# A hybrid decoder block: the causal mask inside the stick-breaking scan, and the short convolution summed by chunk in PSUM

## The chip, the cores and the metric

The kernel runs on one core of a Trainium2 chip. The metric is the device time of one launch in microseconds; the time of a version is the median of its plain runs, and one further run is taken with the profiler on. Engines are called TensorE (PE in the profile; PEld is its weight load), VectorE (DVE), ScalarE (ACT), GpSimd (POOL) and SyncE (SP, which only issues DMAs here). SBUF is the on-chip memory, PSUM the eight banks into which TensorE writes.

## The reference, cut to what matters

One decoder layer on 1,024 tokens plus 16 meta tokens, width 1,024, all in float32. The part that the change touches:

```
xn = rms_norm(h)
b, c, hh, q, k, v, g_conv, g_attn = split(xn @ w_in)
y_conv = b * causal_dwconv(c * hh, conv_w_mix)        # 3 taps per channel
# attention, per head, blocks of queries, keys s < t only:
z        = q k^T / 8
log_fail = where(s < t, log_sigmoid(z) - z, 0)        # log(1 - sigmoid(z))
survive  = cumsum of log_fail from the right, exclusive
a        = where(s < t, exp(log_sigmoid(z) + survive), 0)
o        = a @ v
merged = sigmoid(g_conv + b0) * (y_conv @ w_proj_conv) + sigmoid(g_attn + b1) * (o @ w_proj_attn)
h = h + rms_norm(merged @ w_out)
```

Then a gated MLP, whose up-projection passes through a second causal depthwise convolution of three taps, and `h = h + rms_norm(mlp)`. In products, an attention weight is `sigmoid(z_ts)` times all `1 - sigmoid(z_tj)` for `s < j < t`; so the kernel takes `fl = sigmoid(-z)`, a running product of it from the right, and `be = sigmoid(z)`.

## The kernel before

**Stages.** A first stretch (to about 60 us) normalises the tokens and transposes them into `xnT` (features on partitions). The long second stage, to about 985 us, interleaves two kinds of work. Third, the rest of the gates, the two branch projections, the output projection; fourth, the MLP. Every float32 product is made of three products in the rounded format `float32r` (high by high, high by low, low by high), so operands are split in two: ScalarE casts the high half (L64), and VectorE, or GpSimd for weights, subtracts it for the low half (L65). The operand names ending in `hi`/`lo` or `h`/`l` are these halves.

**Dense items** (class `Dense`). An item is a block of 128 output columns of `w_in`, computed for three chunks of 342 token columns. A chunk is 24 matmuls (L124 to L126) into one PSUM bank of the pool `ps_mm`, which has three banks under the tag `mm`; then its `evac` function takes the result out. When an item starts, the weights of the next one are split: cast on ScalarE, subtraction on GpSimd (`wlo`). The weights after that are loaded by SP. Per head pair the items are `c`, `h`, `b` (the convolution branch: `items_conv`), one gate, and `v`, `q`, `k` of the next pair.

**The convolution.** `evac_c` (L272) copies `c` to SBUF, `evac_h` (L276) multiplies it chunk by chunk with `h` straight from PSUM, and after the third chunk `conv3` (L196 to L198) runs over all 1,026 columns at once, in SBUF: one ScalarE pass with the weight of the third tap, and two VectorE passes `yy = cc * w + yy` for the other two. `evac_b` (L283) multiplies `yy` by `b` and stores it.

**Attention** runs in units of a pair, a head and three blocks of 114 queries. `stage1` makes the scores of a block (L325, L326; up to three pieces of PSUM), the two sigmoids on ScalarE (L327 for `fl`, L328 for `be`), and one step later calls `weights`: VectorE sets the `fl` of masked keys to 1 by a maximum with the tile `ones_up` over the last 114 columns (L335), and scans the block from the right (L336: state = fl * state, minimum with fl). GpSimd multiplies `be` by the scanned `fl`, shifted by one (L338), zeroes the masked part (L339) and pads (L344). `stage2` transposes the weights by TensorE into two PSUM banks called `tp` (L372), splits them into `ah` (ScalarE) and `al` (VectorE), and multiplies by the values (L362, L363). At its end the two halves of the sum are added: ScalarE copies one to `otmp` (L389), VectorE adds (L390). The values are transposed through the same `tp` banks, split into `vv`.

**What sets the order.** A loop written by hand takes steps of `stage1` and `stage2` by planned costs and spends dense steps between them in proportion, so TensorE's order is fixed in advance. On each engine instructions run in the order of its queue, and the compiler's scheduler may place an instruction of another stream between two of the source. Tiles come from pools with a fixed number of buffers; a tile waits until its buffer's last user is done.

**Small tiles.** `par` holds per-channel constants, 106 columns: convolution weights of the mixer (24), gate biases (16) and convolution weights of the MLP (66). It is loaded on SP after the first tokens and weights (L471). The first stretch takes its scalars from a pool `p0s` with four buffers. In the output projection SP loads `g_post` (L683) and `g_pre` (L684), and VectorE multiplies each product by `g_post` (L712).

Of the kernel before, what the change touches and what calls it, by code (L numbers as in the profile page):

```python
# [8 lines left out]
F32 = mybir.dt.float32  # L9
F32R = mybir.dt.float32r  # L10
AF = mybir.ActivationFunctionType
ALU = mybir.AluOpType
PSUM = bass.MemoryType.PSUM

P = 128
# [4 lines left out]
NT = 1040  # L20
NQ = NT - T0
CH = NQ // 3
# [10 lines left out]
def block_kernel(ctx, tc, x, meta_tokens, g_pre_mix, w_in, channels, w_proj_conv,  # L33
# [4 lines left out]
    def pool(name, bufs=1, side="left", space=None):  # L38
        kw = dict(name=name, bufs=bufs, reuse_waits="tile")
        if space is not None:  # L40
            kw["space"] = space
        else:
            kw["side"] = side
        return tc.tile_pool(**kw)
# [3 lines left out]

    ident = const.tile([P, P], F32, name="ident")
    make_identity(nc, ident)  # L50
    par = const.tile([P, 106], F32, name="par")

    o_d = tc.dram_tile([D, NQ], F32, name="o_d")
    y_d = tc.dram_tile([D, NQ], F32, name="y_d")
# [100 lines left out]
    def col_block(w, c):  # L155
# [9 lines left out]
    xnt_ctx = ctx.enter_context(ExitStack())  # L165
    xnt_pool = xnt_ctx.enter_context(pool("xnt"))
    xnT = xnt_pool.tile([P, 2, KB, NT], F32R, name="xnT")
    ones_up = xnt_pool.tile([QB, QB], F32, name="ones_up")
    nc.gpsimd.memset(ones_up, 0.0)
    nc.gpsimd.affine_select(out=ones_up, in_=ones_up, pattern=[[-1, QB]], compare_op=ALU.is_gt,  # L170
                            fill=1.0, base=0, channel_multiplier=1)

    def to_features(dst_hi, dst_lo, src, n, pp):
        for j in range(2):
# [11 lines left out]
    def w_mix(k, b):  # L186
        return par[:, k * 8 + b:k * 8 + b + 1]
# [2 lines left out]
        return par[:, 24 + k * 8 + b:24 + k * 8 + b + 1]  # L190

    def w_ffn(k, b):
        return par[:, 40 + k * NFF + b:40 + k * NFF + b + 1]

    def conv3(dst, src, n, wt):
        nc.scalar.activation(dst, src[:, 2:2 + n], AF.Copy, scale=wt(2))  # L196
        nc.vector.scalar_tensor_tensor(dst, src[:, 1:1 + n], wt(1), dst, op0=ALU.mult, op1=ALU.add)
        nc.vector.scalar_tensor_tensor(dst, src[:, 0:n], wt(0), dst, op0=ALU.mult, op1=ALU.add)  # L198
# [67 lines left out]
    def items_conv(cb):  # L266
        st = {}

        def evac_c(ci, a, n, ps):
            if ci == 0:  # L270
                st["c"] = work.tile([P, NT], F32, name="cc", tag="wk", bufs=4)
            nc.scalar.copy(st["c"][:, a - 12:a - 12 + n], ps)  # L272

        def evac_h(ci, a, n, ps):
            c = st["c"][:, a - 12:a - 12 + n]
            nc.vector.tensor_tensor(c, c, ps, op=ALU.mult)  # L276
            if ci == 2:
                st["y"] = work.tile([P, NT], F32, name="yy", tag="wk", bufs=4)
                conv3(st["y"][:, :NQ], st["c"], NQ, lambda k: w_mix(k, cb))

        def evac_b(ci, a, n, ps):
            y = st["y"][:, a - T0:a - T0 + n]
            nc.vector.tensor_tensor(y, y, ps, op=ALU.mult)  # L283
            if ci == 2:
                nc.sync.dma_start(y_d[cb * P:(cb + 1) * P, :], st["y"][:, :NQ])

        return [(col_block(w_in, 8 + cb), src_x, CH_C, evac_c),
                (col_block(w_in, 16 + cb), src_x, CH_C, evac_h),
                (col_block(w_in, cb), src_x, CH_Q, evac_b)]
# [20 lines left out]
    def stage1(p, h, g):  # L310
# [3 lines left out]
        for b in range(3 * g, 3 * g + 3):  # L314
# [17 lines left out]
                if c0 < nk:  # L332
                    yield n
            def weights(fl=fl, be=be, nk=nk):
                nc.vector.tensor_tensor(fl[:, nk - QB:nk], fl[:, nk - QB:nk], ones_up, op=ALU.max)  # L335
                nc.vector.tensor_tensor_scan(fl[:, :nk][:, ::-1], fl[:, :nk][:, ::-1],  # L336
                                             fl[:, :nk][:, ::-1], 1.0, op0=ALU.mult, op1=ALU.min)
                nc.gpsimd.tensor_tensor(be[:, 0:nk - 1], be[:, 0:nk - 1], fl[:, 1:nk], op=ALU.mult)  # L338
                nc.gpsimd.affine_select(out=be[:, nk - QB:nk], in_=be[:, nk - QB:nk],  # L339
                                        pattern=[[-1, QB]], compare_op=ALU.is_gt, fill=0.0,  # L340
                                        base=0, channel_multiplier=1)
                pad = min(P * (-(-nk // P)), nk_end)
                if pad > nk:
                    nc.gpsimd.memset(be[:, nk:pad], 0.0)  # L344
# [7 lines left out]
    def stage2(p, h, g):  # L352
# [31 lines left out]
        if (h, g) == (0, 0):  # L384
            OT[p] = work.tile([P, NT], F32, name="ot", tag="wk", bufs=4)
        ot = OT[p]
        tmp = work.tile([P, CH], F32, name="otmp", tag="otmp")
        a, b = (0, 64) if h == 0 else (64, 0)
        nc.scalar.copy(tmp[a:a + 64], av[b:b + 64])  # L389
        nc.vector.tensor_tensor(ot[a:a + 64, CH * g:CH * (g + 1)], av[a:a + 64], tmp[a:a + 64],  # L390
                                op=ALU.add)
        if (h, g) == (1, 2):
            nc.sync.dma_start(o_d[p * P:(p + 1) * P, :], ot[:, :NQ])
        yield unit
# [32 lines left out]
        chunk(1, 9)  # L427

    with ExitStack() as p0:
        small = p0.enter_context(pool("p0s", 4, "right"))  # L430
        gb = work.tile([P, NT], F32, name="gb", tag="wk", bufs=4)[:, :D]
        junk = work.tile([P, NT], F32, name="junk", tag="wk", bufs=4)[:, :D]
        warm = small.tile([P, 1], F32, name="warm", bufs=1)
        nc.vector.memset(warm, 1.0)
        nc.scalar.activation(warm, warm, AF.Sqrt)

# [31 lines left out]
        x_load(2)  # L468
        dense.load(0)
        dense.load(1)  # L470
        nc.sync.dma_start(par, channels)  # L471
        start_items(x_block)


# [196 lines left out]
    nc.gpsimd.memset(xr[1][:, :, NQ - 2 * HALF[0][1]:], 0.0)  # L671
    early = x_ctx.enter_context(pool("early"))
    ops = {name: early.tile([P, 2, 4, NJ], F32R, name=f"op{name}") for name in ("B11", "T1")}

    o_ctx = ctx.enter_context(ExitStack())
    osml = o_ctx.enter_context(pool("osml", 4))
# [556 lines left out]
```

## Time and profile before

| | |
|---|---|
| plain runs, median of 3 | 2073.58 us (2072.39 to 2075.9) |
| the profiled execution | 2082.49 us, of which the program's span is 2080.6 us |
| granted TensorE clock over the span | 0.989 |
| stage from 60 to 985 us: TensorE busy | 894.2 of 925 us |
| the same stage: VectorE, ScalarE, GpSimd busy | 535.7, 455.9, 387.1 us |
| `yy` passes on VectorE, first and second tap (x8 each) | 25.2 and 10.2 us |
| mask and scan on VectorE in that stage (x142 each) | 56.5 and 204.5 us |

The profile lists, for groups of instructions of one line, engine and operand names, the busy time in us, the mean of one in ns, and behind a bar the idle time just before them with what ended it. The timeline gives start and duration in us, and in brackets the idle time of that engine before the instruction and the engine, tile and line that ended it. Names such as `tp<-ident,be` are output and inputs. A matmul's end is modelled, so consecutive matmuls overlap in it. The chain is the work that ended last, followed back step by step.

### The profile page before, as it was taken

Reading aid. Unit: us, or ns where it says so; the run is one execution under the profiler, and the core shown is the slowest. Engines: PE = TensorE matmul, PEld = TensorE weight load, DVE = VectorE, ACT = ScalarE, POOL = GpSimd, SP = SyncE. Lnnn points to the kernel's source line nnn. Section 1 sums busy time; section 2 is a strip of 40 time slices with the busy share of each in tenths; the row PEclk is TensorE's granted clock in tenths of the full one; section 3 lists DMA queues with packets and bytes.
Section 4 is the critical chain, followed back from the end, with each engine's and each line's share of the span. In section 5 each row is a group of like instructions: output and inputs, shape, how many; then the busy total and the mean of one; then the engine's idle time right before and its main releaser. Section 6 shows DMA issues by size and latency. Waiting matters only on the chain.

```text
span 2080.6 us, 30846 instructions
## 1 busy us (share of the span) xinstructions
PE 1990.9 (96%) x12228; PEld 1861.3 (89%) x12228; DVE 1076.3 (52%) x1689; ACT 851.0 (41%) x1771; POOL 900.2 (43%) x764
## 2 busy tenths in 40 slices
PE   5999999999999999999999989979999999999997
PEld 4999998998999999999999989978898899878886
DVE  6455565655556565654342114785444444445546
ACT  4444454545445454544441213354334434412122
POOL 4343443434344434434212551225655555555353
PEclk9999999999999999999999999989999999999999
DMA  3111101111111101111375674313222122253323
GB/s 134 41 51 41 61 32 51 42 41 52 41 51 42 61 31 52 41 41 61 124 241 173 170 197 132 104 52 102 77 86 82 62 101 66 77 182 102 101 81 132
DMA packets 56029, 177.57 MB, mean 85 GB/s; under 512 B 12728, under 2 KB 12728, under 8 KB 55884
## 3 DMA queue, kind: packets, MB, share of 16 engines
q1 hardware_dynamic: 52560, 165.09, 24.5%
q10 hardware_dynamic: 3324, 10.50, 1.6%
q8 instruction: 96, 1.57, 0.3%
q14 instruction: 49, 0.40, 0.1%
HBM read 131.36 MB, written 44.21 MB: 84 GB/s over the span
## 4 chain that ended last, share of the span: by engine, by line
PE 80%; DVE 9%; ACT 3%; DMA 3%; POOL 2%; issue 2%; DVEq 0%; ACTq 0%; SPq 0%; POOLq 0%
PE mm L124 13%; PE mm L125 12%; PE mm L126 12%; PE st L861 6%; PE st L865 6%; PE st L863 6%; PE st L1155 3%; PE st L1153 3%; PE st L1154 3%; PE tp L372 3%; PE av L362 2%; PE av L363 2%; PE z L326 2%; PE z L325 2%; DVE fl L336 2%
## 5 line engine op out<-in xcount | busy, mean ns | idle before, releaser
L124 PE MATMUL mm<-xnT,whi 128*128 128x342 f32 (+2 forms) x1536 | 506.6, 330 | 3.6 <-ACT xnT L64 3.6
L125 PE MATMUL mm<-xnT,whi 128*128 128x342 f32 (+2 forms) x1536 | 495.4, 323 | 0.5 <-DVE xnT L65 0.5
L126 PE MATMUL mm<-xnT,wlo 128*128 128x342 f32 (+2 forms) x1536 | 492.2, 320 | 0.0
L338 POOL TENSOR_TENSOR be<-be,fl 114x127 f32<-114x127 f32 (+2 forms) x144 | 177.1, 1230 | 412.0 <-DVE fl L336 187.0
L124 PEld LDWEIGHTS mm<-xnT,whi 128*128 128x128 f32 x1536 | 291.0, 190 | 8.4 <-ACT xnT L64 4.1
L125 PEld LDWEIGHTS mm<-xnT,whi 128*128 128x128 f32 x1536 | 291.7, 190 | 2.2 <-DVE xnT L65 1.0
L126 PEld LDWEIGHTS mm<-xnT,wlo 128*128 128x128 f32 x1536 | 290.9, 189 | 0.0
L65 POOL TENSOR_TENSOR wlo<-raw,whi 128x1024 fp32r<-128x1024 f32 x80 | 201.6, 2520 | 187.2 <-ACT whi L64 175.6
L65 POOL TENSOR_TENSOR a_op<-raw,a_op 128x512 fp32r<-128x512 f32 (+1 forms) x136 | 192.2, 1426 | 89.4 <-ACT a_op L64 86.7
L336 DVE TENSOR_TENSOR_SCAN fl<-fl 114x128 f32<-114x128 f32 (+2 forms) x144 | 209.0, 1451 | 4.9
L65 DVE TENSOR_TENSOR al<-tp,ah 128x342 fp32r<-128x342 f32 (+4 forms) x288 | 127.0, 450 | 139.7 <-ACT ah L64 137.6
L64 ACT CAST ah<-tp 128x342 fp32r<-128x342 f32 (+4 forms) x288 | 113.1, 398 | 194.2 <-PE tp L372 185.8
L861 PE MATMUL st<-opT,a_op 128*128 128x258 f32 (+2 forms) x528 | 171.9, 325 | 4.7 <-ACT snap L876 1.7
L863 PE MATMUL st<-opT,a_op 128*128 128x258 f32 (+2 forms) x528 | 169.8, 322 | 2.9 <-DVE opT L65 2.0
L865 PE MATMUL st<-opT,a_op 128*128 128x258 f32 (+2 forms) x528 | 169.3, 321 | 0.0
L327 ACT ACTIVATE fl<-z 114x348 f32<-114x348 f32 (+10 forms) x240 | 111.5, 465 | 131.9 <-PE z L326 124.5
L64 ACT CAST a_op<-raw 128x512 fp32r<-128x512 f32 (+1 forms) x136 | 85.0, 634 | 156.2 <-DMA raw<-in_w_up_gate_dram 51.2
L372 PE MATMUL tp<-ident,be 114*128 114x114 f32 x720 | 119.7, 263 | 29.5 <-DVE al L65 25.1
L1160 DVE TENSOR_TENSOR acc<-acc,st 128x512 f32<-128x512 f32 x144 | 98.5, 687 | 91.2 <-PE st L1155 91.2
L372 PEld LDWEIGHTS tp<-ident,be 114*128 114x128 f32 x720 | 89.0, 138 | 44.6 <-DVE al L65 34.3
L863 PE MATMUL st<-opB,a_op 128*128 128x512 f32 (+2 forms) x396 | 127.4, 322 | 0.0
L861 PE MATMUL st<-opB,a_op 128*128 128x512 f32 (+2 forms) x396 | 127.3, 321 | 0.0
(172 smaller groups left out, 4408.8 us busy)
## 6 DMA issues: line engine op xcount, KB each, us to landing
raw<-in_w_in_dram SPq DMA_DIRECT2D x64, 512.0 KB
raw<-in_w_up_gate_dram SPq DMA_DIRECT2D x44, 512.0 KB
act_d<-owork SPq DMA_DIRECT2D x22, 512.0 KB
araw<-act_d SPq DMA_DIRECT2D x22, 512.0 KB
raw<-in_w_down_dram SPq DMA_DIRECT2D x22, 512.0 KB
y_d<-yy SPq DMA_DIRECT2D x8, 513.0 KB
ga_d<-gt SPq DMA_DIRECT2D x8, 513.0 KB
o_d<-ot SPq DMA_DIRECT2D x8, 513.0 KB
```

What stands on the lines that cost most here:

```text
L64: nc.scalar.copy(hi, src)
L65: (lo_engine or nc.vector).tensor_tensor(lo, src, hi.bitcast(F32), op=ALU.subtract)
L124: nc.tensor.matmul(ps, wh, xh, start=(kb == 0), stop=False)
L125: nc.tensor.matmul(ps, wh, xl, start=False, stop=False)
L126: nc.tensor.matmul(ps, wl, xh, start=False, stop=(kb == KB - 1))
L327: nc.scalar.activation(fl[:, c0:c0 + n], z, AF.Sigmoid, scale=-0.125)
L336: nc.vector.tensor_tensor_scan(fl[:, :nk][:, ::-1], fl[:, :nk][:, ::-1], fl[:, :nk][:, ::-1], 1.0, op0=ALU.mult, op1=ALU.min)
L338: nc.gpsimd.tensor_tensor(be[:, 0:nk - 1], be[:, 0:nk - 1], fl[:, 1:nk], op=ALU.mult)
L372: nc.tensor.transpose(tp[:n, QB * j:QB * (j + 1)], blocks[j][0][:, kb * P:kb * P + n], ident[:QB, :QB])
L861: nc.tensor.matmul(ps, wt[:, 0, k], xh, start=start and kb == 0, stop=False, skip_group_check=True)
L863: nc.tensor.matmul(ps, wt[:, 0, k], xl, start=False, stop=False, skip_group_check=True)
L865: nc.tensor.matmul(ps, wt[:, 1, k], xh, start=False, stop=stop and kb == 3, skip_group_check=True)
```

## The change

Four things. (1) The tile `ones_up` of 114 columns becomes `upper` of 1,040 columns, zero but for the last 114, and the scan takes it as its second operand with a maximum in place of the minimum: the mask instruction goes. (2) The mixer's convolution is made chunk by chunk in `evac_h`: ScalarE writes the third tap's product into a bank of the pool `ps_mm`, VectorE adds the second tap in that bank and the first tap from there into `yy`. The buffer of `yy` is taken at the first chunk. (3) The tile `otmp` goes: ScalarE copies straight into `ot`, and VectorE adds in place. (4) `par` is cut to 40 columns; the other 66 are loaded into `par_ffn` by SP at the start of the output projection, ahead of `g_post`; the pool `p0s` has two buffers for four, and the tile `warm` shares a tag in it. `conv3` stays for the MLP.

```
-    par = const.tile([P, 106], F32, name="par")
+    par = const.tile([P, 40], F32, name="par")
...
-    ones_up = xnt_pool.tile([QB, QB], F32, name="ones_up")
-    nc.gpsimd.memset(ones_up, 0.0)
-    nc.gpsimd.affine_select(out=ones_up, in_=ones_up, pattern=[[-1, QB]], compare_op=ALU.is_gt,
-                            fill=1.0, base=0, channel_multiplier=1)
+    upper = xnt_pool.tile([QB, NT], F32, name="upper")
+    nc.gpsimd.memset(upper, 0.0)
+    nc.gpsimd.affine_select(out=upper[:, NT - QB:], in_=upper[:, NT - QB:], pattern=[[-1, QB]],
+                            compare_op=ALU.is_gt, fill=1.0, base=0, channel_multiplier=1)
...
     def w_ffn(k, b):
-        return par[:, 40 + k * NFF + b:40 + k * NFF + b + 1]
+        return par_ffn[:, k * NFF + b:k * NFF + b + 1]
...
         def evac_h(ci, a, n, ps):
             c = st["c"][:, a - 12:a - 12 + n]
             nc.vector.tensor_tensor(c, c, ps, op=ALU.mult)
-            if ci == 2:
+            if ci == 0:
                 st["y"] = work.tile([P, NT], F32, name="yy", tag="wk", bufs=4)
-                conv3(st["y"][:, :NQ], st["c"], NQ, lambda k: w_mix(k, cb))
+            j = ci * CH
+            y, src = st["y"][:, j:j + CH], st["c"][:, j:]
+            acc = ps_mm.tile([P, 512], F32, name="yacc", tag="mm")[:, :CH]
+            nc.scalar.activation(acc, src[:, 2:2 + CH], AF.Copy, scale=w_mix(2, cb))
+            nc.vector.scalar_tensor_tensor(acc, src[:, 1:1 + CH], w_mix(1, cb), acc,
+                                           op0=ALU.mult, op1=ALU.add)
+            nc.vector.scalar_tensor_tensor(y, src[:, 0:CH], w_mix(0, cb), acc,
+                                           op0=ALU.mult, op1=ALU.add)
...
             def weights(fl=fl, be=be, nk=nk):
-                nc.vector.tensor_tensor(fl[:, nk - QB:nk], fl[:, nk - QB:nk], ones_up, op=ALU.max)
                 nc.vector.tensor_tensor_scan(fl[:, :nk][:, ::-1], fl[:, :nk][:, ::-1],
-                                             fl[:, :nk][:, ::-1], 1.0, op0=ALU.mult, op1=ALU.min)
+                                             upper[:, NT - nk:][:, ::-1], 1.0,
+                                             op0=ALU.mult, op1=ALU.max)
...
-        tmp = work.tile([P, CH], F32, name="otmp", tag="otmp")
         a, b = (0, 64) if h == 0 else (64, 0)
-        nc.scalar.copy(tmp[a:a + 64], av[b:b + 64])
-        nc.vector.tensor_tensor(ot[a:a + 64, CH * g:CH * (g + 1)], av[a:a + 64], tmp[a:a + 64],
-                                op=ALU.add)
+        o = ot[a:a + 64, CH * g:CH * (g + 1)]
+        nc.scalar.copy(o, av[b:b + 64])
+        nc.vector.tensor_tensor(o, av[a:a + 64], o, op=ALU.add)
...
-        small = p0.enter_context(pool("p0s", 4, "right"))
+        small = p0.enter_context(pool("p0s", 2, "right"))
...
-        warm = small.tile([P, 1], F32, name="warm", bufs=1)
+        warm = small.tile([P, 1], F32, name="warm", tag="v")
...
-        nc.sync.dma_start(par, channels)
+        nc.sync.dma_start(par, channels[:, :40])
...
+    par_ffn = early.tile([P, 66], F32, name="par_ffn")
+    nc.sync.dma_start(par_ffn, channels[:, 40:])
```

## The prediction, as it was put on record

> **What bounds the kernel now.** I read the page first: which engine is full, and where the chain runs.
>
> ```profile
> PE 1990.9 (96%) x12228; PEld 1861.3 (89%) x12228; DVE 1076.3 (52%) x1689; ACT 851.0 (41%) x1771; POOL 900.2 (43%) x764
> ```
>
> TensorE is busy nearly all the time, so a change on other engines can only pay where TensorE stands still. Hence the next view: what TensorE waited for between 60 and 985 us, the stage in which the eight head pairs are interleaved with the dense items. All that the change touches, bar two small loads, lies there.
>
> ```profile
> PE tp L372 <- DVE al L65: 25.1, 20, 2.6
> PE tp L372 <- DVE vv L65: 4.4, 6, 0.7
> ```
>
> Columns: us in total, times, longest. There is one kind of wait: a transpose of attention weights (`tp`) needs one of two PSUM banks, and the bank is free only when VectorE has taken the low half (`al`, or `vv` for the values) out of it. So the question is what stands ahead of `al` in VectorE's queue. I looked with the timeline at one of the twenty, picking the rows of each engine.
>
> ```profile
> 331.14 1.06 ACT L64 CAST whi<-raw 128x1024 fp32r<-128x1024 f32 x1
> 331.30 0.51 DVE L276 TENSOR_TENSOR cc<-cc,mm 128x342 f32<-128x342 f32 x1
> 332.09 1.15 ACT L196 ACTIVATE yy<-cc,par 128x1026 f32<-128x1026 f32 x1
> 333.01 2.39 POOL L65 TENSOR_TENSOR wlo<-raw,whi 128x1024 fp32r<-128x1024 f32 x1
> 333.28 3.21 DVE L197 SCALAR_TENSOR_TENSOR yy<-cc,par,yy 128x1026 f32<-128x1026 f32 x1 [1.47 <-ACT yy L196]
> 333.83 0.70 ACT L64 CAST ah<-tp 128x342 fp32r<-128x342 f32 x2
> 336.41 0.50 DVE L65 TENSOR_TENSOR al<-tp,ah 128x342 fp32r<-128x342 f32 x1
> 336.96 0.30 PE L372 MATMUL tp<-ident,be 114*100 114x114 f32 x1 [1.57 <-DVE al L65]
> ```
>
> This is the short convolution after the last chunk of an `h` item. ScalarE's pass over 1,026 columns waits behind a weight cast, VectorE waits 1.47 us for it, and then the first of VectorE's two passes takes 3.21 us. `al`, whose input was cast from 333.83 on, starts 2.6 us behind that, and TensorE stands 1.57 us. Why 3.21? The groups by line hold the twin pass of the same size, and the chain holds all places but the first with their price, evenly (these two and five between them):
>
> ```profile
> L197 DVE SCALAR_TENSOR_TENSOR yy<-cc,par,yy 128x1026 f32<-128x1026 f32 x8 | 25.2, 3150 | 11.8 <-ACT yy L196 11.8
> L198 DVE SCALAR_TENSOR_TENSOR yy<-cc,par,yy 128x1026 f32<-128x1026 f32 x8 | 10.2, 1273 | 0.0
> ```
> ```profile
> 217.46 3.21 DVE yy L197
> ...
> 919.81 3.20 DVE yy L197
> ```
>
> Same operands, 3150 against 1273 ns. The first pass runs into GpSimd's weight split (333.01 to 335.40) and ends 1.09 us after it: it stood until GpSimd had finished. The next fence has the counterpart: `vv`, with one operand in PSUM, runs its 0.69 us in the middle of a split. [...]
>
> Most of the other waits have a similar cause, at the value items: two in each of six pairs, the first of them the six `vv` waits above.
>
> ```profile
> 267.59 2.40 POOL L65 TENSOR_TENSOR wlo<-raw,whi 128x1024 fp32r<-128x1024 f32 x1
> 268.36 0.69 DVE L65 TENSOR_TENSOR vv<-tp,vv 128x512 fp32r<-128x512 f32 x1 [2.26 <-ACT vv L64]
> 268.97 1.15 DVE L335 TENSOR_TENSOR fl<-fl,ones_up 114x114 f32<-114x114 f32 x1
> 270.16 1.37 DVE L336 TENSOR_TENSOR_SCAN fl<-fl 114x584 f32<-114x584 f32 x1
> 271.68 1.22 POOL L338 TENSOR_TENSOR be<-be,fl 114x583 f32<-114x583 f32 x1 [1.69 <-DVE fl L336]
> 272.23 0.79 DVE L335 TENSOR_TENSOR fl<-fl,ones_up 114x114 f32<-114x114 f32 x1
> 273.06 1.65 DVE L336 TENSOR_TENSOR_SCAN fl<-fl 114x698 f32<-114x698 f32 x1
> ```
>
> The mask (L335) stands until the split ends at 269.99, then the scan follows; the second mask stands behind GpSimd's product in the same way. And twice (here, and at 476.86) a scan of 1,040 columns just misses its turn: the split starts between mask and scan, and the scan takes 4.40 us.
>
> ```profile
> 352.06 0.37 DVE L335 TENSOR_TENSOR fl<-fl,ones_up 114x114 f32<-114x114 f32 x1 [1.62 <-ACT fl L327]
> 352.27 2.41 POOL L65 TENSOR_TENSOR wlo<-raw,whi 128x1024 fp32r<-128x1024 f32 x1
> 352.46 4.40 DVE L336 TENSOR_TENSOR_SCAN fl<-fl 114x1040 f32<-114x1040 f32 x1
> 357.32 0.42 PE L372 MATMUL tp<-ident,be 114*128 114x114 f32 x2 [1.95 <-DVE al L65]
> 476.86 0.32 PE L372 MATMUL tp<-ident,be 114*128 114x114 f32 x1 [1.90 <-DVE al L65]
> ```
>
> Last, the granted clock behind two of the eight convolution stops (columns from the ninth on: PEclk, DMA share, GB/s):
>
> ```profile
> 338.70:342.10 3.40, 3.40 (x14) 3.36 (x14) 2.51 (x4) 1.35 (x3) 1.11 (x1) 0.50 0.00 0
> 458.17:461.57 3.40, 3.40 (x13) 3.36 (x14) 2.60 (x4) 1.35 (x3) 1.02 (x1) 0.50 0.00 0
> ```
>
> 3.40 us at half clock cost 1.7 us of work each. The two stops behind missed scans (357.32, 476.86) come 15.2 and 15.3 us after the ends of exactly these stretches.
>
> **The change, part by part.** First the convolution. Gone per pair: one ScalarE pass of 1.15 us and VectorE passes of 3.15 and 1.27 us in one piece. New, per chunk of 342 columns, three times: a ScalarE copy into a PSUM bank and two VectorE passes that read one SBUF and one PSUM operand. No row shows ScalarE writing PSUM or this VectorE form; the nearest are these, with the mask's row:
>
> ```profile
> L272 ACT COPY cc<-mm 128x342 f32<-128x342 f32 (+1 forms) x24 | 10.7, 445 | 3.1 <-PE mm L126 3.1
> 114.27 0.32 PE L372 MATMUL tp<-ident,be 114*128 114x114 f32 x1 [1.28 <-DVE al L65]
> ```
> ```profile
> 326.69 0.51 DVE L276 TENSOR_TENSOR cc<-cc,mm 128x342 f32<-128x342 f32 x1 [1.52 <-PE mm L126]
> L335 DVE TENSOR_TENSOR fl<-fl,ones_up 114x114 f32<-114x114 f32 x142 | 56.5, 398 | 93.6 <-ACT fl L327 85.0 <-POOL be L338 6.5
> ```
>
> Bounds: the copy 0.445 to 1.15 us (all 1,026 columns), a pass 0.51 to 1.27 us. I take 0.445 and 0.51, the rows of equal width with one operand in PSUM. Chunks 0 and 1 then cost VectorE 1.0 us each while TensorE has 331.30 - 326.69 = 4.61 us to the next chunk's end; free time hides them. After chunk 2: product until 331.81; the copy still stands behind the cast until 332.09, ends 332.54; two passes to 333.6; the `ah` cast 0.7 us earlier than now; `al` at about 333.7 and out by 334.2. TensorE needs the bank at 336.96 - 1.57 = 335.39, so the stop goes with 1.2 us to spare. What is late next is ScalarE's cast ahead of the copy. Seven stops, taken as 1.57 each, and the first pair's of 1.28 (row at 114.27): **12.3 us**. [...]
>
> Second, the two half-clock stretches, **3.4 us**, and the two missed scans, 1.95 + 1.90 = **3.9 us**. They go if the stops go. [...]
>
> Third, the mask in the scan. 142 instructions of 398 ns leave VectorE, 56.5 us, nearly all beside TensorE's work. On the path they count at the value items. There the first scan starts when the mask's own wait ended (269.99, less what the mask then still took, 0.25): 0.3 us earlier. GpSimd's product starts as much earlier, and the second scan, freed at about 272.5 instead of starting at 273.06, comes 0.6 us earlier: 6 x 0.6 = **3.6 us**. The rest of those waits stays: the split still blocks a scan as it did the mask. A scan that reads a second tile should cost what it does now: at 4.40 us it is already shut out by GpSimd as the mask with its two tiles is. Were the second tile a stream of its own, at the 0.51 us per 342 columns above, a scan of 698 would be 1.0 us longer and the 3.6 and 3.9 lost.
>
> Fourth, what costs nothing with the cover named. Setting a `[114, 1040]` tile instead of a small one, and the later load of 66 columns:
>
> ```profile
> 1.19 0.95 POOL L218 MEMSET ql<- 64x1026 f32 x1
> 9.11 0.45 PE L178 MATMUL tp<-ident,xn 128*128 128x128 f32 x1 [9.11 <-DVE xn L459]
> ```
> ```profile
> 1261.00 0.87 SPq L684 DMA_DIRECT2D g_pre<-in_g_pre_ffn_dram  x1
> 1266.92 0.94 DVE L712 TENSOR_TENSOR row<-po,g_post 114x342 f32<-114x342 f32 x2 [5.70 <-DMA g_post<-in_g_post_mix_dram]
> 1269.10 0.32 PE L704 MATMUL po<-w_o,mb 128*114 128x342 f32 x1
> ```
>
> The memset is some 0.95 us on GpSimd, behind which only other memsets and the identity are queued, and TensorE starts at 9.11 waiting for VectorE. The load goes into SP's queue ahead of `g_post` and `g_pre`; at up to 0.87 us it delays `g_post`, for which VectorE already waits 5.70 us; its first two products are out by 1267.86, and TensorE needs the first bank again at 1269.10, so 1.2 us cover it; without cover it costs 0.9 us, once. The smaller ring of scalar tiles (two instead of four) is in a stretch where VectorE's own order keeps two blocks apart; the direct copy into `ot` keeps engines and shapes, but its first copy waits on ScalarE for that tile's buffer, which VectorE's add did until now.
>
> Sum: 12.3 + 3.4 + 3.9 + 3.6 = 23.2 us for the profiled execution (2082.5 us, span 2080.6). The median of the plain runs is 2073.6, 8.9 us below it, so plain runs may lack the half-clock stretches and what hangs on them (7.3); I count those at half, 3.6. That makes 19.5 us, and **2054.1 us**.
>
> **Rivals.** *The chunk's chain is too slow.* With the upper prices (copy 1.15, passes 1.27) the last pass ends at 332.09 + 1.15 + 2.54 = 335.8, `al` at 336.3, and 0.9 of the 1.57 us stays; the gain is 12.3 - 8 x 0.9 = 5.1, with the scan's 3.6 lost to a longer scan and about 1 from the clock: **2067**. For it: three small passes pay a fixed cost three times. Against: one operand lies in PSUM, as with `al`.
>
> *It doesn't do what it says: the stop passes to the next one in the queue.* If the 698 scan moves up into the place of L197, the split shuts it out until 335.40, it ends 1.6 us later, and `al` is out at 337.5, later than now. Then 12.3 is not gained and 8 x 0.6 is lost, against 3.6 gained: 1 us slower, **2075**, no change. Against: a scan is issued only behind the next block's first scores.
>
> *Slower: the ring runs out.* A third of the dense ring now holds the sum, and VectorE stands at ScalarE's copy 24 times, not 8. The bank must be empty when the next group but one starts, 4.61 us later. Two scans and two passes nearly fill that. If each of 24 groups waits as VectorE did (1.47 us), that is 35 us against 16 gained: **2093**. It decides from 4.61 us on; with 0.5 + 0.45 + 1.0 us of own work it takes two scans ahead of the passes each time.
>
> **How the numbers follow.** Forecast 0.62, slow chain 0.16, stop passed on 0.11, ring 0.11. The range goes down to all of 23.2 plus half of the waits that I left uncounted (29.5 - 19.8, halved: 5), 2045, and up to the slow chain, 2067; the other two lie outside. About 0.2% (4 us) is what a measurement of this kernel can tell from no change. Faster by more: 0.62 + 0.16 = 0.78; within: 0.11; slower: 0.11.
>
> **What would show it.** Right: L197 and L198 at about 0.5 us each, x24, beside GpSimd's split too; no `PE tp <- DVE al` at the end of `h` items; that row down from 25.1 to 10 us or less; no L335; scan durations as now. Wrong: TensorE waiting at L124 for a bank held by the sum; scans with long durations where L197 stood; a longer scan; a new half-clock stretch.

## The result, and the profile after

The kernel after takes 2087.74 us (median of 8 runs, 2080.5 to 2091.61), the kernel before 2077.21 us on the same chip (8 runs, 2072.39 to 2083.7): a ratio of 1.0055, 95% interval 1.0039 to 1.0072. It is slower by half a per cent where 1% faster was forecast, and outside the range. The profiled execution takes 2085.2 us (span 2083.4), that of before 2082.49 (2080.6).

The page's first part, of after:

```profile
PE 1991.2 (96%) x12228; PEld 1865.4 (90%) x12228; DVE 1041.5 (50%) x1577; ACT 853.4 (41%) x1787; POOL 903.4 (43%) x764
```

VectorE has lost 35 us of work and 112 instructions, as planned, and TensorE is as full as it was. So again the question is what TensorE waits for from 60 to 985 us (us in total, times, longest):

```profile
PE av L371 <- DVE al L65: 15.0, 7, 2.2
PE tp L380 <- DVE al L65: 14.0, 13, 1.6
PE tp L380 <- DVE vv L65: 2.5, 6, 0.4
```

31.5 us, against 29.5 in the two rows of before. The waits have new places, not a smaller sum. The seven in the first row lie where the stops behind the long convolution pass lay, at the end of the `h` items, and are longer: 2.1 to 2.2 us each for 1.6. Of the 13 in the second row, seven of 1.5 to 1.6 us stand behind a scan of 1,040 columns; before there were two of those. Six of 0.5 and the six of the third row are the value items. They did get shorter.

The new copy and passes themselves cost a little more than was forecast (0.445 and 0.51 us). Groups by line of after (busy us, mean ns, then the idle time before them):

```profile
L283 ACT ACTIVATE yacc<-cc,par 128x342 f32<-128x342 f32 x24 | 13.3, 552 | 1.4 <-DVE cc L277 1.4
```
```profile
L284 DVE SCALAR_TENSOR_TENSOR yacc<-cc,par,yacc 128x342 f32<-128x342 f32 x24 | 13.7, 569 | 10.0 <-ACT yacc L283 10.0
L286 DVE SCALAR_TENSOR_TENSOR yy<-cc,par,yacc 128x342 f32<-128x342 f32 x24 | 13.4, 559 | 0.4
```

Now the end of an `h` item, the place that the prediction read at 331 us. Timeline of after, rows of each engine:

```profile
333.30 0.55 ACT L283 ACTIVATE yacc<-cc,par 128x342 f32<-128x342 f32 x1
333.88 2.40 POOL L65 TENSOR_TENSOR wlo<-raw,whi 128x1024 fp32r<-128x1024 f32 x1
333.88 0.58 DVE L284 SCALAR_TENSOR_TENSOR yacc<-cc,par,yacc 128x342 f32<-128x342 f32 x1 [0.87 <-ACT yacc L283]
334.37 3.38 DVE L343 TENSOR_TENSOR_SCAN fl<-fl,upper 114x698 f32<-114x698 f32 x1
334.46 0.51 ACT L64 CAST ah<-tp 128x228 fp32r<-128x228 f32 x2
337.67 0.54 DVE L286 SCALAR_TENSOR_TENSOR yy<-cc,par,yacc 128x342 f32<-128x342 f32 x1
338.14 0.56 DVE L65 TENSOR_TENSOR al<-tp,ah 128x228 fp32r<-128x228 f32 x2
338.57 0.37 PE L371 MATMUL av<-al,vv 128*128 128x228 f32 x1 [2.12 <-DVE al L65]
```

The chunk's chain starts as forecast: L284 runs its 0.58 us in the first half of a weight split (333.88 to 336.28). Then, between the two passes, stands a scan of 698 columns. Both its inputs lie in SBUF, as those of L197 did, and it stands as that did: it takes 3.38 us, where the 698 scans with no split beside them take 1.58 to 2.13 in this trace, and ends 1.47 us behind the split. L286 and `al` queue behind it, and TensorE stands 2.12 us. VectorE's queue at this place, as the compiler laid it out (before, then after; operations of one chunk's end):

```
before: cc  yy(L197)  al  yy(L198)  al  al  yy*b(L283)  mask  scan 698
after:  cc  yacc(L284)  scan 698  yy(L286)  al  al  ot  yy*b(L291)
```

In the source the scan comes behind the transposes of the unit in both. The place between two dependent passes was not empty before either: there the scheduler had put the `al` of 336.41 (in seven pairs), and in the first pair the mask of a scan. Rows of before:

```profile
109.27 0.27 DVE L335 TENSOR_TENSOR fl<-fl,ones_up 114x114 f32<-114x114 f32 x1
...
336.83 1.27 DVE L198 SCALAR_TENSOR_TENSOR yy<-cc,par,yy 128x1026 f32<-128x1026 f32 x1
```

So the change did not make this place; another instruction came into it, in seven of eight pairs the scan. Why the scheduler chose the scan is not shown.

The second new stop, 19 us later. First after, then, for comparison, a version that has only the small edits of the change (experiment 1), where this scan wins in every pair:

```profile
350.79 1.82 POOL L346 TENSOR_TENSOR be<-be,fl 114x925 f32<-114x925 f32 x1 [2.09 <-DVE fl L343]
352.55 0.46 ACT L335 ACTIVATE fl<-z 114x344 f32<-114x344 f32 x1
352.69 0.28 POOL L347 TENSOR_SCALAR_AFFINE_SELECT be<-be 114x114 f32<-114x114 f32 x1
352.94 2.38 POOL L65 TENSOR_TENSOR wlo<-raw,whi 128x1024 fp32r<-128x1024 f32 x1
353.11 4.40 DVE L343 TENSOR_TENSOR_SCAN fl<-fl,upper 114x1040 f32<-114x1040 f32 x1 [1.64 <-ACT fl L335]
357.97 0.51 PE L380 MATMUL tp<-ident,be 114*128 114x114 f32 x3 [1.54 <-DVE al L65]
```
```profile
349.14 1.83 POOL L339 TENSOR_TENSOR be<-be,fl 114x925 f32<-114x925 f32 x1 [2.08 <-DVE fl L337]
350.43 0.46 ACT L328 ACTIVATE fl<-z 114x344 f32<-114x344 f32 x1
351.00 0.28 DVE L336 TENSOR_TENSOR fl<-fl,ones_up 114x114 f32<-114x114 f32 x1 [1.60 <-POOL be L339]
351.05 0.37 POOL L340 TENSOR_SCALAR_AFFINE_SELECT be<-be 114x114 f32<-114x114 f32 x1
351.31 2.33 DVE L337 TENSOR_TENSOR_SCAN fl<-fl 114x1040 f32<-114x1040 f32 x1
351.39 4.44 POOL L65 TENSOR_TENSOR wlo<-raw,whi 128x1024 fp32r<-128x1024 f32 x1
```

With the mask, the scan starts 0.08 us ahead of the split, takes its 2.33, and the split takes 4.44 in its place, which nobody waits for. Without the mask, GpSimd's product of the block before (L346) ends 0.40 us ahead of the last sigmoid instead of 0.08 us behind it (352.61 against 353.01; 350.97 against 350.89): with the mask's part of the change alone it is 0.39, experiment 2. It can begin sooner, I take it, because the scan ahead of it has no mask to wait for. So the split starts 0.17 us ahead of the scan, and the scan takes 4.40. In before and after it goes by which of the two starts first: the five scans of 1,040 that start 0.07 to 0.08 us ahead of a split take 2.32 or 2.33 us and those splits 4.43 or 4.44; the nine that start 0.11 to 0.19 us behind one take 4.39 to 4.46 and those splits 2.38 to 2.41. By form, the groups of the two sizes, before and after, 60 to 985 us:

```profile
L336 DVE TENSOR_TENSOR_SCAN fl<-fl 114x1040 f32<-114x1040 f32 x15 | 39.0, 2600 | 0.5
L336 DVE TENSOR_TENSOR_SCAN fl<-fl 114x698 f32<-114x698 f32 x16 | 27.1, 1691 | 0.5
```
```profile
L343 DVE TENSOR_TENSOR_SCAN fl<-fl,upper 114x1040 f32<-114x1040 f32 x15 | 50.9, 3394 | 11.6 <-ACT fl L335 6.5 <-POOL be L347 4.8
L343 DVE TENSOR_TENSOR_SCAN fl<-fl,upper 114x698 f32<-114x698 f32 x16 | 41.3, 2579 | 3.7 <-ACT fl L335 3.7
```

Last, the granted clock. Before has three half-clock stretches of 3.4 us in the stage, after has six, one at each of six of the seven stops at the `h` items. Windows of the profile of after (length, busy time of the five engines with counts, granted clock, DMA):

```profile
335.50:338.91 3.41, 1.29 (x9) 1.05 (x8) 3.20 (x4) 0.00 (x0) 1.80 (x2) 1.00 0.42 153
338.91:342.32 3.41, 3.41 (x15) 3.40 (x14) 1.01 (x2) 0.46 (x2) 0.80 (x3) 0.50 0.00 1
...
693.84:697.25 3.41, 1.83 (x12) 1.83 (x13) 2.01 (x5) 0.44 (x1) 1.83 (x3) 1.00 0.52 159
697.25:700.66 3.41, 3.41 (x24) 3.40 (x23) 1.22 (x3) 1.82 (x4) 0.00 (x0) 1.00 0.00 0
```

In these two traces every change of the recorded clock lies a whole number of 3.413 us behind the first one; the windows are laid on that grid. In the window before the first, TensorE was busy for 1.29 us, so it stood 2.12, and the next window runs at half clock. The stop of 2.12 us that ended at 695.42 is cut by the grid: 1.58 us of standing in its window, and the clock stays. Cut in this way, the traces of before, after and the twelve versions below say the same: each of 27 windows with 1.8 us or more of standing is followed by one at half clock; of 27 with 1.5 to 1.75 us two are, both in before (the two that the prediction quoted); of 3,726 with less, none.

Three more stretches of 3.41 us at a clock of 0.50 are 5.1 us of work, and the waits are 2 us more: 7.1 together. The last scan of the stage starts 7.6 us later (1002.44 against 994.85). The two profiled executions as a whole differ by only 2.8 us, because between 985 and 2070 us before stood at half clock for 20.5 us and after for 10.2, in stages that the change hardly touches. The plain medians differ by 10.5 us: 7.6 of them lie in the stage, by one execution of each, and for the other 3 there is no account.

### The profile page after: what moved, and what is told of

The parts are those of the page before. It is cut to its first block, busy times and chain, and to the rows that moved or that the text cites. A ratio compares the mean times of both kernels' runs of the same rounds, so it can differ in the third digit from the quotient of the medians.

```text
span 2083.4 us, 30757 instructions
## 1 busy us (share of the span) xinstructions
PE 1991.2 (96%) x12228; PEld 1865.4 (90%) x12228; DVE 1041.5 (50%) x1577; ACT 853.4 (41%) x1787; POOL 903.4 (43%) x764
## 3 DMA queue, kind: packets, MB, share of 16 engines
q8 instruction: 96, 1.57, 0.3%
## 4 chain that ended last, share of the span: by engine, by line
PE 74%; DVE 11%; DMA 5%; ACT 4%; POOL 3%; issue 2%; ACTq 0%; DVEq 0%; SPq 0%; POOLq 0%
PE mm L124 13%; PE mm L125 12%; PE mm L126 12%; PE st L870 5%; PE st L872 5%; PE st L874 5%; DVE fl L343 4%; PE st L1164 3%; PE st L1162 3%; PE st L1163 3%; PE tp L380 3%; PE av L370 2%; PE av L371 2%; POOL a_op L65 2%; DMA xv<-in_x_dram 2%
## 5 line engine op out<-in xcount | busy, mean ns | idle before, releaser
L124 PE MATMUL mm<-xnT,whi 128*128 128x342 f32 (+2 forms) x1536 | 508.9, 332 | 3.6 <-ACT xnT L64 3.6
L346 POOL TENSOR_TENSOR be<-be,fl 114x127 f32<-114x127 f32 (+2 forms) x144 | 177.5, 1233 | 399.5 <-DVE fl L343 324.0
L343 DVE TENSOR_TENSOR_SCAN fl<-fl,upper 114x128 f32<-114x128 f32 (+2 forms) x144 | 242.3, 1684 | 126.0 <-ACT fl L335 113.3
L124 PEld LDWEIGHTS mm<-xnT,whi 128*128 128x128 f32 x1536 | 292.6, 191 | 8.3 <-ACT xnT L64 4.0
L65 POOL TENSOR_TENSOR wlo<-raw,whi 128x1024 fp32r<-128x1024 f32 x80 | 191.6, 2395 | 201.3 <-ACT whi L64 201.3
L872 PE MATMUL st<-opB,a_op 128*128 128x512 f32 (+2 forms) x396 | 127.3, 322 | 1.9 <-DVE opB L65 1.9
L870 PE MATMUL st<-opB,a_op 128*128 128x512 f32 (+2 forms) x396 | 127.2, 321 | 0.0
L874 PE MATMUL st<-opB,a_op 128*128 128x512 f32 (+2 forms) x396 | 126.9, 320 | 0.0
```

The costliest lines, as they stand in the source:

```text
L65: (lo_engine or nc.vector).tensor_tensor(lo, src, hi.bitcast(F32), op=ALU.subtract)
L124: nc.tensor.matmul(ps, wh, xh, start=(kb == 0), stop=False)
L870: nc.tensor.matmul(ps, wt[:, 0, k], xh, start=start and kb == 0, stop=False, skip_group_check=True)
L872: nc.tensor.matmul(ps, wt[:, 0, k], xl, start=False, stop=False, skip_group_check=True)
L874: nc.tensor.matmul(ps, wt[:, 1, k], xh, start=False, stop=stop and kb == 3, skip_group_check=True)
```

## The experiments

Three theories stood at first. **A**: what costs TensorE time is which VectorE instruction with both inputs in SBUF stands ahead of `al` while GpSimd's weight split runs, and so has to stand until the split has ended. (What the expectations call the port is a name for this standing, in after 3.38 us for 2.13 or less and 4.40 for 2.33; what lies behind it is shown by no run.) **B**, the prediction's third rival: the sum in a PSUM bank of the dense ring is itself slow. And one that the small edits cost the 10 us. All ratios are to the kernel before, run beside on the same chip; before took 2066.6 to 2068.8 us on these chips, so medians are compared within a line alone. A ratio is not quite the quotient of two medians; the two differ by up to 0.15%. Waits are TensorE's for `al` and `vv`, and half-clock stretches are those from 60 to 985 us, both of the profiled execution.

| version | median us | ratio, 95% interval | waits us | half clock |
|---|---|---|---|---|
| 1 small edits only | 2067.53 | 0.9989 (0.9964 to 1.0013) | 25.1 | 1 |
| 2 and the mask in the scan | 2068.72 | 1.0000 (0.9978 to 1.0022) | 27.6 | 1 |
| 3 small edits and the convolution | 2086.22 | 1.0089 (1.006 to 1.0118) | 31.6 | 5 |
| 4 after, split in pieces | 2050.22 | 0.9907 (0.9874 to 0.994) | 6.7 | 0 |
| 5 before, split in pieces | 2054.65 | 0.9934 (0.9918 to 0.9949) | 14.6 | 1 |
| 6 after, scan 698 behind `al` | 2060.49 | 0.9956 (0.9944 to 0.9968) | 17.4 | 0 |
| 7 after, GpSimd delayed | 2065.03 | 0.9986 (0.9975 to 0.9996) | 21.5 | 2 |
| 8 both 6 and 7 | 2045.02 | 0.9884 (0.9871 to 0.9896) | 6.5 | 0 |
| 9 after, once more | 2080.87 | 1.0068 (1.0052 to 1.0085) | 31.5 | 6 |
| 10 both 4 and 6 | 2043.05 | 0.9882 (0.9869 to 0.9894) | 2.5 | 0 |
| 11 version 2, GpSimd delayed | 2056.03 | 0.9946 (0.9933 to 0.9959) | 17.6 | 1 |
| 12 version 6, 1,040 stops made longer | 2063.9 | 0.9986 (0.9976 to 0.9996) | 21.9 | 3 |

**1 to 3: the parts alone.** Of the change, 1 takes back (a) and (b) below, 2 only (a), 3 only (b).

```
 (a)
-            acc = ps_mm.tile([P, 512], F32, name="yacc", tag="mm")[:, :CH]
...
+            if ci == 2:
+                conv3(st["y"][:, :NQ], st["c"], NQ, lambda k: w_mix(k, cb))
 (b)
+                nc.vector.tensor_tensor(fl[:, nk - QB:nk], fl[:, nk - QB:nk], ones_up, op=ALU.max)
...
-                                             upper[:, NT - nk:][:, ::-1], 1.0,
-                                             op0=ALU.mult, op1=ALU.max)
+                                             fl[:, :nk][:, ::-1], 1.0, op0=ALU.mult, op1=ALU.min)
```

> The changed kernel with the old mask instruction and the old convolution: only the direct copy into ot, the later load of 66 columns, the smaller ring of scalars. Theory A (what counts is which two-input VectorE instruction stands ahead of al while GpSimd's weight split holds the shared read port): VectorE's queue has the same order as before, so the time is that of before, ratio 0.998 to 1.002. Theory B (the sum in a PSUM bank of the dense ring is itself slow): the same, as the sum is not in it. A theory that the small edits cost the 10 us: ratio 1.005.

> The changed kernel with the old convolution over 1,026 columns; the mask is in the scan. Theory A: the eight stops behind the long convolution pass stay at about 1.6 us; the two waits at each value item shrink from 1.9 to about 0.7 us a pair (-7 us); the scan of 1,040 columns now loses the port to the weight split in most pairs, 4.4 us for 2.3 (+1.9 us in six or seven pairs, +12 us): 2076 to 2086 us, ratio 1.000 to 1.005. Theory B: only the gain of the scan, 2070 us, ratio 0.997.

> The changed kernel with the old mask instruction; the convolution is summed by chunk in PSUM. Theory A: in VectorE's queue the scan of 698 columns stands behind the two al, but its mask instruction ahead of them, held by the weight split: a stop of 1 to 1.6 us per pair as before, the scan of 1,040 as before; 2072 to 2080 us, ratio 0.997 to 1.002. Theory B: slower by as much as the whole change, 2087 us, ratio 1.005, with TensorE waiting at L124 for a bank.

The small edits cost nothing that can be seen, and the third theory falls. The mask's part alone is no gain: its value items' waits are as short as in after (2.5 us, six, in the row of `vv`), but the scan of 1,040 loses in all seven pairs. The convolution alone is the slow part, and this missed A's expectation of 0.997 to 1.002. Its waits:

```profile
PE tp L380 <- DVE al L65: 19.4, 15, 1.9
PE av L371 <- DVE al L65: 7.9, 7, 1.1
```

The stops at the `h` items are shorter (here the mask of the 698 scan stands between the two passes, held by the split, 2.36 us for 0.28), much as A said; the seven at the 1,040 scan I had not expected, since the mask is still there. The trace has them by 0.1 us: GpSimd's product ends 0.06 us ahead of the last sigmoid (349.61 against 349.67) where it ended 0.08 us behind it in version 1. With five half-clock stretches the sum is there without theory B, and TensorE has no wait at L124 (a bank held by the sum) in the stage. A's mechanism held and its forecast of one race did not.

**4 and 5: the split in four pieces**, in after and in before. The work is the same; a piece of 256 columns would take about 0.6 us, an estimate from the 2.40 us of the whole.

```
-                split(hi, lo, raw, nc.gpsimd)
+                nc.scalar.copy(hi, raw)
+                for q in range(4):
+                    s = slice(q * D // 4, (q + 1) * D // 4)
+                    nc.gpsimd.tensor_tensor(lo[:, s], raw[:, s], hi[:, s].bitcast(F32), op=ALU.subtract)
```

> The changed kernel, GpSimd's weight split of 1,024 columns issued in four pieces of 256, so that the port is held for about 0.65 us at a time: the queue of VectorE is the same as in the changed kernel. Theory A: the scans of 3.4 and 4.4 us fall to at most 2.3 and 3.0, the seven stops of 2.4 and the seven of 1.9 us nearly go, and the half-clock stretches behind them: 2055 to 2068 us, ratio 0.990 to 0.996. Theory B: no effect, 2087 us, ratio 1.005.

> The kernel before, with the weight split on GpSimd in four pieces of 256 columns instead of one of 1024. Theory A (what costs TensorE its time is a two-input VectorE instruction shut out by that split, whichever instruction the queue puts there): the long convolution pass and the scans wait at most about 0.6 us instead of 2.4, the seven stops of 1.57 us and the two of 1.9 go, and so does most of the half clock: some 12 + 4 + 3 of 2080 us, ratio 0.989 to 0.995, TensorE's waits at the weight transposes under 12 us from 25. The change is then worth little beside it, since the same kernel with the change stood at 0.9907. Rival (the change has a gain of its own that only the port hid): 0.996 to 1.000, so that the change is worth some 0.7% once the split is in pieces.

The same place at the end of the `h` item in version 4 (VectorE, then GpSimd):

```profile
327.03 0.58 DVE L287 SCALAR_TENSOR_TENSOR yacc<-cc,par,yacc 128x342 f32<-128x342 f32 x1 [0.87 <-ACT yacc L286]
327.51 1.72 DVE L346 TENSOR_TENSOR_SCAN fl<-fl,upper 114x698 f32<-114x698 f32 x1
329.16 0.54 DVE L289 SCALAR_TENSOR_TENSOR yy<-cc,par,yacc 128x342 f32<-128x342 f32 x1
...
327.03 4.12 POOL L112 TENSOR_TENSOR wlo<-raw,whi 128x256 fp32r<-128x256 f32 x4
```

The scan is still in front of L289, and takes 1.72 us instead of 3.38; the four pieces give way to it and take 4.12 together. B is refuted: the sum in PSUM is all there, and the kernel is 0.9% faster than before. The pieces help before too (0.9934), so much of the gain is theirs and not the change's. Both came inside A's ranges. These two intervals overlap, and with the pieces alone the change's share can't be told from none.

**6 to 8: each stop by itself.** In 6 the 698 scan of the first head is queued behind the last `al` that precedes it in the source (an edge of order in VectorE's queue, no wait). In 7 GpSimd does more: it repeats the select of the 926 block twice (in 16 blocks, not the 14 that the expectation names).

```
 (6)
+                behind = last.get("al") if nk == 698 and h == 0 else None
+                with (tc.issue_after(behind.ins) if behind is not None else ExitStack()):
...
 (7)
+                for _ in range(3 if nk == 926 else 1):
...
```

> The kernel after, with one thing changed: the scan of 698 columns of the first head is queued behind the attention weights' last split (al) that stands ahead of it in the source, so that it no longer stands between the two convolution passes. Theory A: the seven stops of 2.3 us at the end of the h items go (-14 to -16 us) and with them the half clock that begins 1.7 us behind each (six stretches, up to -8); the scans of 1040 stay shut out seven times (1.75 us each). Ratio to the kernel before 0.994 to 1.000, against 1.0055 with the scan in front. Rival (the order does not matter, the scan's price only moves: it then holds GpSimd's product and the next transposes as long): 1.003 to 1.007.

> The kernel after with work added: GpSimd repeats the masking select of the 926-column block twice (two more of about 0.25 us each, 14 blocks, the result unchanged), so that the weight split that follows in its queue starts about 0.5 us later. Theory A (the scan of 1040 loses the port by 0.1 to 0.2 us, because without the mask GpSimd is done that much sooner): the scan now comes first, takes 2.3 us instead of 4.4, and the seven stops of 1.75 us go: -12 us, with perhaps a little of the half clock; the h-end stops stay. Ratio to the kernel before 0.997 to 1.002. Rival (the scan of 1040 is late by itself, and the split is not what it waits for): GpSimd's added 7 us change nothing or cost, 1.005 to 1.008.

> Both edits: the 698 scan queued behind al, and GpSimd delayed by two repeated selects at the 926 block; the weight split stays in one piece. Theory A: both kinds of stops go, 16 + 12 us, and the half clock with them; about the time that the split in four pieces gave, ratio to the kernel before 0.988 to 0.995. Rival (a split in one piece costs something else besides, so the pieces did more than win these two places): 0.996 to 1.002.

All three as theory A has it, in time and in place. TensorE's waits for `al` in 6, in 7, and in 8 (the `vv` row is 2.5 us in each, as in after):

```profile
PE tp L382 <- DVE al L65: 14.9, 14, 1.6
```
```profile
PE av L372 <- DVE al L65: 15.0, 7, 2.2
PE tp L381 <- DVE al L65: 4.0, 7, 1.0
```
```profile
PE tp L383 <- DVE al L65: 4.0, 7, 1.0
```

The order edge removes the row `av` and nothing else; the delay removes the 1,040 stops and nothing else; both leave 6.5 us, `vv` included. (In 6 the waits have one more of 1.0 us: it is the last one, which in after lies behind 985 us.) In 6 VectorE's rows are those that the prediction had drawn, and L286 follows L284 at once:

```profile
330.11 0.58 DVE L284 SCALAR_TENSOR_TENSOR yacc<-cc,par,yacc 128x342 f32<-128x342 f32 x1 [0.87 <-ACT yacc L283]
330.72 0.57 DVE L286 SCALAR_TENSOR_TENSOR yy<-cc,par,yacc 128x342 f32<-128x342 f32 x1
331.21 0.57 DVE L65 TENSOR_TENSOR al<-tp,ah 128x228 fp32r<-128x228 f32 x2
331.70 2.29 DVE L345 TENSOR_TENSOR_SCAN fl<-fl,upper 114x698 f32<-114x698 f32 x1
```

And in 7 added work makes the kernel faster than after: GpSimd's three selects, of about 0.28 us each alone, take 2.88 us here and end 0.06 us behind the scan, and the split follows with no scan beside it (GpSimd, VectorE):

```profile
349.86 2.88 POOL L348 TENSOR_SCALAR_AFFINE_SELECT be<-be 114x114 f32<-114x114 f32 x3
352.72 2.40 POOL L65 TENSOR_TENSOR wlo<-raw,whi 128x1024 fp32r<-128x1024 f32 x1
```
```profile
350.28 2.40 DVE L343 TENSOR_TENSOR_SCAN fl<-fl,upper 114x1040 f32<-114x1040 f32 x1 [1.64 <-ACT fl L335]
```

**9 to 11: after again, the two best remedies together, and the mask's part priced.** 10 joins the edits of 4 and 6; 11 is version 2 with the repeated selects of 7.

> The kernel after, unchanged, on the chip of the two runs beside it. Theory A says nothing new: 1.004 to 1.007, seven stops behind the 698 scan and seven behind the 1040 scan in the profile. A rival (the loss belongs to the chip or the run in which it was first measured, and the races fall otherwise elsewhere) would give 0.995 to 1.002 and fewer lost scans of 1040.

> The kernel after with both remedies: the weight split in four pieces, and the 698 scan queued behind al. Theory A: of the 6.7 us that TensorE still waited with the pieces alone, the 3.4 behind the 698 scan go; ratio 0.987 to 0.990 against 0.9907 with the pieces alone. Rival (the two remedies do the same, and the pieces have taken all there is): 0.990 to 0.992.

> The kernel after with the old convolution in one pass at the end (so only the mask's part of the change stays), and with GpSimd's two repeated selects at the 926 block. It prices the mask's part with the lost scans of 1040 taken out. Theory A: the seven stops of about 1.57 us behind the long pass stay, those behind the 1040 scans go, the value items' waits fall by about 3.6 us as predicted: ratio 0.994 to 0.999, against 1.000 without the selects. Rival (the mask's part is worth nothing even so, and all the gain lies in the convolution): 0.999 to 1.001.

The loss is there again, with the same 14 stops and six half-clock stretches. 10 is as fast as 8 and the fastest seen; against the pieces alone (0.9907) its interval overlaps, but its profile has lost the row `av`, as expected. Against 5, the kernel before with the same pieces, it stands clear: 0.9882 to 0.9934. And 11, inside its range, prices the parts with the lost races taken out: from 1 to 11 the mask's part is worth 0.0043 x 2067 = 9 us, from 11 to 8 the convolution 0.0062 x 2067 = 13 us. The three were run on three chips, each against before on its own; by their intervals the 9 is good to some 6 us either way and the 13 to some 4.

**12: the clock by itself.** Version 6 has no half clock in the stage and seven stops of 1.57 us. Here VectorE applies the mask twice more behind the 1,040 scan of the first head.

```
+                if nk == 1040 and h == 0:
+                    for _ in range(2):
+                        nc.vector.tensor_tensor(fl[:, nk - QB:nk], fl[:, nk - QB:nk],
+                                                upper[:, NT - QB:], op=ALU.max)
```

> The version with the 698 scan queued behind al (0.9956, no half clock in the stage, seven stops of 1.57 us behind the 1040 scans), with work added on VectorE: behind the scan of 1040 columns of the first head the mask is applied twice more (2 x 0.28 us, the result unchanged), ahead of al. The stops become about 2.1 us. Theory of the clock, from the traces so far: it is set for windows of 3.413 us on a fixed grid; 24 of 24 windows in which TensorE stood 1.8 us or more were followed by one at half clock, 2 of 26 with 1.5 to 1.7 us, none below. So stops of 2.1 us now fall wholly enough into one window in about 4 of 7 cases (3 to 6), and the time goes up by 7 x 0.5 + 4 x 1.7 = 10 us: ratio 0.999 to 1.003, and each half-clock window follows a window with 1.8 us or more of standing. Rival (the clock goes by something else, such as two stops some 20 us apart): at most one stretch, +3.7 us, ratio 0.996 to 0.999.

The stops became 2.2 us and three half-clock stretches came, the lowest number named, each behind a window with 1.98 us or more of standing. Two of the seven places, one that fell and one that did not (1.43 and 1.67 us busy):

```profile
349.47:352.88 3.41, 1.43 (x11) 1.13 (x8) 3.34 (x4) 0.99 (x2) 1.34 (x3) 1.00 0.44 154
352.88:356.29 3.41, 3.23 (x13) 3.17 (x14) 1.07 (x3) 0.79 (x2) 2.15 (x2) 0.50 0.00 0
697.62:701.03 3.41, 1.67 (x12) 1.36 (x10) 3.34 (x4) 0.99 (x2) 1.46 (x2) 1.00 0.45 154
701.03:704.44 3.41, 2.97 (x22) 2.94 (x23) 1.84 (x4) 0.89 (x2) 2.31 (x2) 1.00 0.00 0
```

The plain time, 0.9986, fell a hair under the range written for the clock's theory and inside the rival's, so the time alone does not decide. In the profile the last scan of the stage starts 9.1 us later than in 6 (985.55 against 976.46), near the 10 that was written; by the ratios the plain runs are 6 us longer than those of 6, give or take 3. It is the places of the stretches that tell the two apart. There are no two stops 20 us apart in this kernel.

## Why the prediction was wrong

**The step that failed** is the dismissal of the second rival: "Against: a scan is issued only behind the next block's first scores." That holds for the source. Yet the queue of VectorE is the scheduler's, and it put the scan between L284 and L286. In the sum the step is "two passes to 333.6", which lets the second pass follow the first at once: it began 3.2 us behind the first one's end, since the scan stood there for 3.38. That something could stand there was to be seen in before, where `al` or a mask stood between L197 and L198 in every pair. The rival's own working is nearly what came: "the split shuts it out until 335.40, it ends 1.6 us later"; the stop came out at 2.1 us, and it had a chance of 0.11. It also put the price too low, as it counted this stop alone.

By the terms of the sum, from the profiled executions (us of TensorE's time, minus is gain):

| term | forecast | came | shown by |
|---|---|---|---|
| convolution stops, first pair with them | -12.3 | +3.9 at the seven, -2.4 in the first pair | 6: seven gone; 11 to 8: -13 |
| lost scans of 1,040 | -3.9 | +7.1 (two to seven) | 7: seven gone |
| value items | -3.6 | -4.1 (9.5 to 5.5) | 2, 11 |
| half clock | -3.4 | +5.1 (three to six) | 6 and 8: none; 12 |

The forecast had left out a last wait of 2.6 us near 975 us, with the third half-clock stretch behind it; in after this wait is 1.0 and lies beyond the window. With it these rows make the 2 us of waits and the 5.1 of the clock.

**Right** were the prices: the copy 0.55 and the passes 0.57 and 0.56 us (0.445 and 0.51 taken), the passes with one PSUM operand kept their length beside the split (0.58 us at 333.88, inside its 2.40; 0.54 to 0.58 over all 48), the scan costs the same with its second tile (2.33 us for 1,040 when free), the value items, and nothing seen for the small edits. The ring of banks never ran out: TensorE has no wait at L124 in the stage. The six new passes take 3.4 us a pair, against 2.5 for two free passes over 1,026 columns, and with the scan out of the way (6, 8) TensorE waits for none of it. In version 8, where both stops are gone, 0.9884 is 24 us of gain where the sum was 23.2. That the totals meet is in part luck, for the parts do not all: the convolution's 13 for 12.3 is the same term, but the mask's part measures 9 for 3.6, though its interval reaches down to that. From 1 to 11 the traces show 4.0 us less waiting at the value items, and 2.1 less at the seven stops behind the long pass and 1.6 less at the last wait near 970 us, which the forecast had not counted.

**Wrong** beside the queue was "They go if the stops go", of the two missed scans. The row that would have told it was in the trace of before. A scan of 1,040 that won there (VectorE, then GpSimd):

```profile
235.04 2.33 DVE L336 TENSOR_TENSOR_SCAN fl<-fl 114x1040 f32<-114x1040 f32 x1
...
235.12 4.44 POOL L65 TENSOR_TENSOR wlo<-raw,whi 128x1024 fp32r<-128x1024 f32 x1
```

0.08 us is no settled order, when the edit takes a mask of 0.28 us out of what stands ahead of it. In version 1, with before's mask and convolution, none of the seven lost, where before had lost two. I priced the two scans that lost and took the other five as safe.

The clock was sized by two stops of 1.57 and 1.59 us that it followed, taken for the rule. Over all traces they are the exceptions (2 of 27), and why the clock fell behind those two stays open; what to count in these traces are the windows of 3.413 us with 1.8 us or more of standing (27 of 27 were followed by half clock), and the change made seven stops long enough for one, of 2.1 to 2.2 us.

## What to carry over

Before counting on an instruction's place, read the queue that the compiler builds, since the scheduler may put an instruction of another stream between two dependent ones, and an edit can change which one comes there. Where an instruction of one engine stands while one of another runs, as the scan of 1,040 did beside a split (4.40 us for 2.33), list every such pair that is close and how close: here an edit that removed a mask of 0.28 us turned all five races that before had won by 0.07 or 0.08 us. The safer remedy is to cut the instruction that the other stands for into pieces (0.9907 for 1.0055 here) or to make the order explicit (0.9956), and to price the edit afterwards.

## What was not expected of the hardware

More work made the kernel faster: 32 repeated selects of about 0.28 us brought after from 1.0055 and 1.0068 to 0.9986. A split in four pieces that a scan comes between takes 4.12 us in place of 2.40, and costs nothing that shows. And the granted clock of TensorE changed on a fixed grid of 3.413 us: the stop of 2.12 us that one window held (335.50 to 338.91) was followed by 3.41 us at 0.50, which is 1.7 us of work, and the stop of 2.12 us that the grid cut in two (1.58 us in the window from 693.84) by 1.00.
